# Gathering the rows of a mixture-of-experts stage by indirect DMA instead of by one-hot products

## The chip, the cores and the metric

The kernel runs as one program on one core of a Trainium2 chip. The metric is the device time of one execution in microseconds. Before the change three runs took 2869.97, 2870.82 and 2877.7 us, with a median of 2870.82 us.

## The reference, cut to what matters

The reference is two transformer-like blocks on 512 tokens of width 1024. The change touches only the last stage, the mixture of experts. Its routing picks two experts of 32 for each token, and only the chosen ones have a weight other than zero in `combine`:

```python
for e in range(N_EXPERTS):                       # 32 experts
    he = jax.nn.silu(t @ w_g[e]) * (t @ w_u[e])  # t: 512 x 1024, w_g and w_u: 1024 x 256
    out = out + combine[:, e:e + 1] * (he @ w_d[e])   # w_d: 256 x 1024
```

After it come the residual and a last normalisation. All inputs and outputs are float32. Each expert has 3 x 1024 x 256 weights, 3.15 MB, so the 32 experts have 100.7 MB that are read once.

## The kernel before, in words

The stage starts from two tiles that lie feature-major, `hT` (the residual) and `nT` (the normalised input of the experts), each 128 partitions by 8 blocks by 512 tokens. `tail2` (from L2257) computes the router's logits, and `choose` and `places` find for each token its two experts, their weights (`cmb`) and the token's place in each expert's list (`pos`, 0 to 63 for the 64 slots of an expert; an expert with more tokens is handled by `overflow`, under a condition that is read from the data). `token_major` transposes `nT` back to token-major on TensorE, and `split` (L2267 to L2270) turns each half of a block of 128 tokens into a high part `n2h` (ScalarE) and a remainder `n2l` (VectorE), both fp32r. `plain` does a plain copy of `hT` into `yac`, on which the experts' results are added.

`experts` (from L2073) runs over eight groups q of four experts. In each:

- Four VectorE comparisons make `oh`, a one-hot matrix of 512 tokens by 256 slots (L2081).
- The slots get their tokens' rows as a product: for each of eight feature blocks and four token blocks there is one matmul with `n2h` and one with `n2l` (L2093, L2094), 64 in all, with 256 columns each. `xg` receives the result from PSUM, two blocks at a time, half of the copies on ScalarE and half on VectorE (L2095). `xg` is double-buffered over q.
- Then two pairs of experts follow. In a pair the two experts stand beside each other in TensorE's columns (64 each). Four small matmuls with `chl` fetch the slots' weights (L2106), `w2` is made of them on VectorE, 16 fp32 matmuls that the trace shows as 32 instructions compute gate and up (L2118), then come Silu (L2122), four transposes of `oh` (L2125) and the copy `ohT`, the product with the weights `h` (L2128), two transposes of `h` (L2131) and the copy `hT` (L2133), and eight matmuls with the down weights (16 instructions, L2141). Their result is scaled and split into `yh` and `yl` (L2144 to L2146).
- At the end of the group, 32 matmuls with `ohT` (L2155, L2156) bring both pairs' results back to the tokens, and VectorE adds them to `yac` (L2157).

The weights come through `load` (L2053 on), in tiles of 1 MB, nine buffers (`EW`), and six tiles per pair: the first half of the rows of gate and up for each expert, the second half, and the down matrix. Tile j takes the buffer of tile j - 9: the first three tiles of a pair wait for the matmuls with down of the pair two before, the last three for the gate and up matmuls of the pair before. The DMAs are issued by SyncE, in program order, on one queue. In the gate and up loads partition p receives the rows k * 128 + p, so each run in memory is one row of 256 floats, 1 KB. A down row is 4 KB.

The order of instructions on each engine is chosen when the program is built, by a planner that goes by priorities (the order in the source) and by a timeline of its own. Every engine then executes its instructions in that order. PSUM has eight banks, here four of `pa`, three of `pb` and one of `pf`. TensorE instructions are called PE in the rows, VectorE DVE, ScalarE ACT, GpSimd POOL; SPq is SyncE's sequencer.

Of the kernel before, what the change touches and what calls it, by code (L numbers as in the profile page):

```python
# [20 lines left out]
D = 1024  # L21
# [9 lines left out]
L = 512  # L31
# [391 lines left out]
def constants():  # L423
    f = np.float32
    k = {"k_ident": np.eye(128, dtype=f)}
    s4 = np.zeros((128, 32), f)
    for j in range(4):
        s4[32 * j + np.arange(32), np.arange(32)] = 1
    k["k_sel4"] = s4
    t = np.arange(768)  # L430
    k["k_rst64"] = np.broadcast_to((t % 64 != 0).astype(f), (128, 768)).copy()
    dm = np.zeros((128, 2, 6, 32), f)
    s = np.arange(128)[:, None] % 32
    q = np.arange(32)[None, :]
# [35 lines left out]
    k["k_iota"] = np.broadcast_to(np.arange(64, dtype=f), (128, 64)).copy()  # L470
    inv = (10000.0 ** (-np.arange(0, 64, 2, dtype=np.float64) / 64)).astype(f)
    k["k_invf"] = np.tile(inv, 4)[:, None].copy()
    return k
# [1478 lines left out]
CAP = 64  # L1952
THR = CAP
EW = 9
GT = "pf"
G0 = "pa"


class Moe:
# [72 lines left out]
    def route(self, pool):  # L2032

        nc = self.nc
        t = lambda n, s: pool.tile([128, 4] + list(s), F32, name=n)
# [12 lines left out]
        self.chl = pool.tile([128, 4, 16, 2, 2], F32R, name="chl")  # L2048
# [4 lines left out]
    def load(self, i, ew, j):  # L2053


        nc = self.nc
        if j >= NE * 3 or j in self.ewt:
            return
        e, part = j // 6 * 2 + j % 2, j % 6 // 2
        t = ew.tile([128, 2048], F32, name="ew", bufs=EW).rearrange("p (k n) -> p k n", k=2 if part == 2 else 4)  # L2060
        rows = lambda w: i[w][0][e].rearrange("(k p) n -> p k n", p=128)
        if part < 2:
            for n, w in enumerate(("w_exp_gate_2", "w_exp_up_2")):
                nc.sync.dma_start(t[:, :, n * 256:n * 256 + 256], rows(w)[:, part * 4:part * 4 + 4])
        else:
            nc.sync.dma_start(t, rows("w_exp_down_2"))
# [6 lines left out]
    def experts(self, i, ew, n2h, n2l, yac, xg2, g2, yhl):  # L2073

        nc, tc = self.nc, self.tc
        with tc.tile_pool(name="eb", bufs=1, reuse_waits="tile") as eb:
            batch = []
            for q in range(8):
                oh = eb.tile([128, 4, 256], F32R, name="oh", bufs=2)
                for c in range(4):  # L2080
# [4 lines left out]
                xg = xg2[:, q % 2]  # L2085
                for k2 in range(4):
                    p = self.pt(GT if q else G0)
                    for kk in range(2):
                        k = k2 * 2 + kk
                        ks = slice(k * 128, (k + 1) * 128)  # L2090
                        o = p[:, kk * 256:kk * 256 + 256]
                        for c in range(4):
                            nc.tensor.matmul(o, n2h[:, c, ks], oh[:, c, :], start=(c == 0), stop=False)  # L2093
                            nc.tensor.matmul(o, n2l[:, c, ks], oh[:, c, :], start=False, stop=(c == 3))  # L2094
                    (nc.vector.tensor_copy if k2 % 2 else nc.scalar.copy)(  # L2095
                        xg[:, k2 * 2:k2 * 2 + 2, :], p.rearrange("p (a s) -> p a s", a=2))
                for pr in range(2):
                    e0 = q * 4 + pr * 2
                    for j in range(e0 * 3, e0 * 3 + 6):
                        self.load(i, ew, j)  # L2100
                    wts = [self.ewt.pop(j) for j in range(e0 * 3, e0 * 3 + 6)]
                    ss = slice(pr * 128, pr * 128 + 128)

                    pw = self.pt("pb")
                    for c in range(4):
                        nc.tensor.matmul(pw[:, :4], oh[:, c, ss], self.chl[:, c, e0 // 2].rearrange("p a b -> p (a b)"),  # L2106
                                         start=(c == 0), stop=(c == 3))
                    w2 = eb.tile([128, 1], F32, name="w2", bufs=2)
                    w4 = eb.tile([128, 4], F32, name="w4", bufs=2)
                    nc.vector.tensor_copy(w4, pw[:, :4])  # L2110
                    for x in range(2):
                        rs = slice(x * 64, x * 64 + 64)
                        nc.vector.tensor_add(w2[rs, :], w4[rs, x:x + 1], w4[rs, 2 + x:3 + x])

                    ph = self.pt("pa")
                    for k in range(8):
                        for x in range(2):
                            nc.tensor.matmul(ph[x * 64:x * 64 + 64, :], xg[:, k, pr * 128 + x * 64:pr * 128 + x * 64 + 64],  # L2118
                                             wts[k // 4 * 2 + x][:, k % 4, :], start=(k == 0), stop=(k == 7),
                                             tile_position=(0, x * 64))  # L2120
                    h = eb.tile([128, 256], F32, name="h", bufs=2)
                    nc.scalar.activation(h, ph[:, :256], AF.Silu)  # L2122
                    pt_ = self.pt("pb")
                    for c in range(4):
                        nc.tensor.transpose(pt_[:, c * 128:(c + 1) * 128], oh[:, c, ss].bitcast(F32), self.ident)  # L2125
# [109 lines left out]
class Tail:  # L2235
# [3 lines left out]
    def tail1(self, i, mo, mn, ys, x1d, g2d, ths):  # L2239
# [9 lines left out]
        for name, shape in (("tri8", [128, 64]), ("triu", [128, 128]), ("iota", [128, CAP_])):  # L2249
# [7 lines left out]
    def tail2(self, i, mo, out):  # L2257
        nc, tc = self.nc, self.tc
        rt = mo.tile([128, 4, 36], F32, name="rt")
        n2h, n2l = self.slot("n2h", "Q", True), self.slot("n2l", "A", True)  # L2260
        yac = self.slot("yac", "B", True, F32)
        self.ewt = {}
        with tc.tile_pool(name="ea", bufs=1, reuse_waits="tile") as ea:
# [1 line left out]
            logits = self.logits(i, mo, self.nT, rt)  # L2265

            def split(p, c, f):  # L2267
                fs = slice(f * 512, f * 512 + 512)
                nc.scalar.copy(n2h[:, c, fs], p)
                nc.vector.tensor_sub(n2l[:, c, fs], p, n2h[:, c, fs].bitcast(F32))  # L2270

            def plain(p, c, f):
                (nc.vector.tensor_copy if f else nc.scalar.copy)(yac[:, c, f * 512:f * 512 + 512], p)
# [16 lines left out]
            xg = self.mo.tile([128, 2, 8, 256], F32, name="xg", tag="P", bufs=1)  # L2290
            self.experts(i, ea, n2h, n2l, yac, xg, self.g2, yhl)
            self.finish(mo, yac, self.slot("yg", "Q", True, F32), self.fg, out)


# [256 lines left out]
```

## Time and profile before

| | |
|---|---|
| median of three runs | 2870.82 us |
| profiled execution, its own time | 2875.16 us |
| its span, first to last instruction | 2873.4 us |
| busy share of the span: PE, PEld, DVE, ACT, POOL | 95%, 73%, 54%, 35%, 9% |
| TensorE's mean granted clock | 0.98 |
| moved by DMA | 374.20 MB, mean 130 GB/s |
| loads of `ew` (gate, up: 64 DMAs of 512 KB each) | 9.9 and 8.8 us from issue to landing |
| loads of `ew` (down: 32 DMAs of 1024 KB) | 11.0 us from issue to landing |

PE is a matmul, PEld the load of its stationary operand, which overlaps with other matmuls. Matmuls overlap in the records, since they are pipelined: the distance between two starts, not the length of one, is what a matmul costs in a row of them. The expert stage is the last 350 us of the span; its PE is busy without a gap from 2525 to 2825 us.

### The profile page before, as it was taken

How to read it: one execution, taken by the hardware profiler on the slowest of the kernel's cores; microseconds unless marked ns; L12 is line 12 of the kernel's file. 1: busy time of each engine (PE TensorE's matmuls, PEld its weight loads, DVE VectorE, ACT ScalarE, POOL GpSimd, SP SyncE). 2: the span in 40 equal slices, each digit the busy share in tenths (PEclk: the TensorE clock that was granted, in tenths of full speed). 3: DMA queues.
4: the chain of work that ended last, by engine and by line, in shares of the span. 5: the costliest groups of instructions: out<-in, count | busy, mean ns of one | idle time of the engine just before them, and what ended most of it. 6: DMA issues, size and time to landing. Idle time of an engine off the chain costs nothing. (4 is left out here: it accounts for less than half of the span.)

```text
span 2873.4 us, 41502 instructions
## 1 busy us (share of the span) xinstructions
PE 2731.4 (95%) x16545; PEld 2099.0 (73%) x16546; DVE 1551.9 (54%) x3009; ACT 996.1 (35%) x1791; POOL 264.2 (9%) x303
## 2 busy tenths in 40 slices
PE   7999999999998878999999999999999999999997
PEld 5788888888787766688887778777667668854553
DVE  6333333348267995544345756676766654633334
ACT  5211111235235663322224424565444532311112
POOL 2000000002002220100000101121222220000000
PEclk9999999999999998999999999999999999999999
DMA  7422212224333237633324433202333475478885
GB/s 260 146 88 66 67 54 65 66 82 119 108 89 90 64 121 258 228 103 94 92 85 124 119 99 87 63 13 61 86 105 103 137 248 162 137 252 294 289 296 190
DMA packets 387125, 374.20 MB, mean 130 GB/s; under 512 B 20329, under 2 KB 316653, under 8 KB 386674
## 3 DMA queue, kind: packets, MB, share of 16 engines
q1 hardware_dynamic: 386930, 371.53, 41.2%
q8 instruction: 131, 2.15, 0.3%
q14 instruction: 64, 0.52, 0.1%
HBM read 343.94 MB, written 27.53 MB: 129 GB/s over the span
## 5 line engine op out<-in xcount | busy, mean ns | idle before, releaser
L191 ACT CAST whi<-wraw 128x1024 fp32r<-128x1024 f32 x277 | 285.9, 1042 | 748.2 <-PE pppa L211 333.5
L210 PE MATMUL pppa<-lath,whi 128*128 128x512 f32 (+4 forms) x1344 | 522.8, 390 | 19.2 <-ACT whi L191 5.7
L211 PE MATMUL pppa<-latl,whi 128*128 128x512 f32 (+3 forms) x1344 | 519.6, 387 | 5.7 <-DVE latl L358 3.6
L212 PE MATMUL pppa<-lath,wlo 128*128 128x512 f32 (+3 forms) x1344 | 513.6, 384 | 0.5 <-DVE wlo L192 0.4
L192 DVE TENSOR_TENSOR wlo<-wraw,whi 128x1024 fp32r<-128x1024 f32 (+1 forms) x273 | 332.7, 1225 | 253.8 <-ACT whi L191 249.2
L210 PEld LDWEIGHTS pppa<-lath,whi 128*128 128x128 f32 (+3 forms) x1344 | 253.0, 188 | 86.4 <-ACT whi L191 12.3
L211 PEld LDWEIGHTS pppa<-latl,whi 128*128 128x128 f32 (+2 forms) x1344 | 252.8, 188 | 65.9 <-DVE latl L358 6.0
L212 PEld LDWEIGHTS pppa<-lath,wlo 128*128 128x128 f32 (+2 forms) x1344 | 252.3, 188 | 56.5 <-issue 2.8
L211 PE MATMUL pppb<-hl,whi 128*128 128x512 f32 (+1 forms) x576 | 195.4, 341 | 0.0
L210 PE MATMUL pppb<-hh,whi 128*128 128x512 f32 (+1 forms) x576 | 193.4, 345 | 0.0
L212 PE MATMUL pppb<-hh,wlo 128*128 128x512 f32 (+1 forms) x576 | 191.6, 341 | 0.0
L416 DVE SCALAR_TENSOR_TENSOR xT<-pppb,sG,xT 128x512 f32<-128x512 f32 (+1 forms) x144 | 96.8, 690 | 138.2 <-PE pppb L212 138.1
L396 DVE TENSOR_TENSOR hf<-sg,pppa 128x256 f32<-128x256 f32 (+1 forms) x68 | 39.7, 584 | 234.7 <-PE pppa L212 233.4
L210 PE MATMUL pppf<-lath,whi 128*128 128x512 f32 x320 | 129.3, 404 | 5.0 <-ACT whi L191 1.7
L210 PE MATMUL pppa<-ctxh,whi 128*128 128x256 f32 (+1 forms) x440 | 124.8, 284 | 7.9 <-DVE W L918 7.9
L2118 PE MATMUL pppa<-ew,xg 128*64 128x512 f32 x512 | 131.2, 597 | 0.0
L210 PEld LDWEIGHTS pppb<-hh,whi 128*128 128x128 f32 x576 | 108.1, 189 | 28.0 <-issue 5.8
L212 PE MATMUL pppf<-lath,wlo 128*128 128x512 f32 x320 | 127.4, 398 | 0.6 <-DVE wlo L192 0.6
L211 PE MATMUL pppf<-latl,whi 128*128 128x512 f32 x320 | 127.7, 399 | 0.0
L211 PE MATMUL pppa<-ctxl,whi 128*128 128x256 f32 (+1 forms) x440 | 124.6, 283 | 0.2 <-POOL ctxl L356 0.2
L212 PE MATMUL pppa<-ctxh,wlo 128*128 128x256 f32 (+1 forms) x440 | 124.7, 283 | 0.0
L211 PEld LDWEIGHTS pppb<-hl,whi 128*128 128x128 f32 x576 | 108.5, 188 | 16.1 <-issue 3.4
(700 smaller groups left out, 5170.6 us busy)
## 6 DMA issues: line engine op xcount, KB each, us to landing
wraw<-in_ffn_w_dram SPq DMA_DIRECT2D x132, 512.0 KB, 4.1
wraw<-in_w_in_dram SPq DMA_DIRECT2D x102, 512.0 KB, 4.1
ew<-in_w_exp_gate_dram SPq DMA_DIRECT2D x64, 512.0 KB, 9.9
ew<-in_w_exp_up_dram SPq DMA_DIRECT2D x64, 512.0 KB, 8.8
ew<-in_w_exp_down_dram SPq DMA_DIRECT2D x32, 1024.0 KB, 11.0
mraw<-in_w_mod_dram SPq DMA_DIRECT2D x40, 512.0 KB, 6.6
wraw<-in_w_mod_dram SPq DMA_DIRECT2D x32, 512.0 KB, 4.4
mraw<-in_w_ada_dram SPq DMA_DIRECT2D x32, 512.0 KB, 6.7
```

The costliest lines, as they stand in the source:

```text
L191: nc.scalar.copy(hi[:, :n], raw[:, :n])
L192: (nc.gpsimd if pool else nc.vector).tensor_sub(lo[:, :n], raw[:, :n], hi[:, :n].bitcast(F32))
L210: nc.tensor.matmul(out, wh, xh, start=start, stop=False)
L211: nc.tensor.matmul(out, wh, xl, start=False, stop=False)
L212: nc.tensor.matmul(out, wl, xh, start=False, stop=stop)
L396: nc.vector.tensor_mul(h[:, :n], sg[:, :n], pp[1])
L416: nc.vector.scalar_tensor_tensor(x[:, o, :], p[:, :n], gate[:, o:o + 1], x[:, o, :], op0=OP.mult, op1=OP.add)
L2118: nc.tensor.matmul(ph[x * 64:x * 64 + 64, :], xg[:, k, pr * 128 + x * 64:pr * 128 + x * 64 + 64], wts[k // 4 * 2 + x][:, k % 4, :], start= ...
```

## The change

- `split` no longer makes a high part and a remainder. It copies each half block once (ScalarE for the first half, VectorE for the second) into one tile `n2`, with the features reordered on the way, so that feature p * 8 + k lies at k * 128 + p; the writes have a stride of 128 floats. After the second half SyncE stores the block's 128 rows in a DRAM tensor `n2d` (four stores of 512 KB).
- `chl` carries a third value per token besides the two parts of the weight: the token's number, from a new constant `tok`. The small matmuls with `oh` have six columns in place of four and so yield, for each of the 128 slots of a pair, the number of its token. VectorE turns it into an integer, `ix`, and GpSimd issues an indirect DMA which brings the 128 rows (4 KB each) from `n2d` into one of four slots of `xr`. This is `gather(q)`, for both pairs of a group; it is called one group ahead.
- `turn(n)` transposes the gathered rows of pair n in eight 128 by 128 pieces on TensorE into two PSUM banks (`pf` and `pb`), from where ScalarE and VectorE copy them to one of four slots of `xg4`. It stands in the source after the gate and up matmuls of the pair before.
- The 512 one-hot matmuls (L2093, L2094) and their copies are gone.
- In the gate and up loads partition p receives rows p * 8 to p * 8 + 7, four to a tile, so one run in memory is 4 KB. The down loads stay.

```diff
     def load(self, i, ew, j):
...
+            t = t.rearrange("p (n k m) -> p n k m", n=2, k=4)
             for n, w in enumerate(("w_exp_gate_2", "w_exp_up_2")):
-                nc.sync.dma_start(t[:, :, n * 256:n * 256 + 256], rows(w)[:, part * 4:part * 4 + 4])
+                nc.sync.dma_start(t[:, n], i[w][0][e].rearrange("(p k) n -> p k n", k=8)[:, part * 4:part * 4 + 4])
...
+            xr = self.slot("xr", "A", True, F32)
+            def gather(q):
+                oh = eb.tile([128, 4, 256], F32R, name="oh", bufs=2)
...
+                for pr in range(2):
+                    n = q * 2 + pr
+                    pw = self.pt("pb")
+                    for c in range(4):
+                        nc.tensor.matmul(pw[:, :6], oh[:, c, pr * 128:pr * 128 + 128],
+                                         self.chl[:, c, n].rearrange("p a b -> p (a b)"), start=(c == 0), stop=(c == 3))
+                    ix = eb.tile([128, 1], U32, name="ix", bufs=4)
+                    nc.vector.tensor_copy(ix, pw[:, 4:5])
+                    rows[n] = xr[:, n % 4, :]
+                    nc.gpsimd.indirect_dma_start(rows[n], None, n2d, bass.IndirectOffsetOnAxis(ap=ix, axis=0))
...
+            def turn(n):
+                r = rows.pop(n)
+                for f in range(2):
+                    p = self.pt(("pf", "pb")[f])
+                    for k in range(4):
+                        k4 = f * 4 + k
+                        nc.tensor.transpose(p[:, k * 128:(k + 1) * 128], r[:, k4 * 128:(k4 + 1) * 128], self.ident)
+                    (nc.vector.tensor_copy if f else nc.scalar.copy)(
+                        xg4[:, n % 4, f * 4:f * 4 + 4, :], p.rearrange("p (k s) -> p k s", k=4))
+            gather(0)
+            turn(0)
+            for q in range(8):
+                if q < 7:
+                    gather(q + 1)
...
-                for k2 in range(4):
-                    p = self.pt(GT if q else G0)
-                    for kk in range(2):
...
-                            nc.tensor.matmul(o, n2h[:, c, ks], oh[:, c, :], start=(c == 0), stop=False)
-                            nc.tensor.matmul(o, n2l[:, c, ks], oh[:, c, :], start=False, stop=(c == 3))
-                    (nc.vector.tensor_copy if k2 % 2 else nc.scalar.copy)(
-                        xg[:, k2 * 2:k2 * 2 + 2, :], p.rearrange("p (a s) -> p a s", a=2))
...
                     nc.scalar.activation(h, ph[:, :256], AF.Silu)
+                    if e0 < 30:
+                        turn(e0 // 2 + 1)
...
             def split(p, c, f):
-                fs = slice(f * 512, f * 512 + 512)
-                nc.scalar.copy(n2h[:, c, fs], p)
-                nc.vector.tensor_sub(n2l[:, c, fs], p, n2h[:, c, fs].bitcast(F32))
+                (nc.vector.tensor_copy if f else nc.scalar.copy)(
+                    n2[:, c, :].rearrange("p (k q) -> p q k", k=8)[:, f * 64:f * 64 + 64, :],
+                    p.rearrange("p (q k) -> p q k", k=8))
+                if f:
+                    nc.sync.dma_start(n2d[c * 128:(c + 1) * 128, :], n2[:, c, :])
```

## Rows read from the trace of the kernel before

**Rows 1.** The page: busy us (share of the span) and instructions of each engine.
```profile
PE 2731.4 (95%) x16545; PEld 2099.0 (73%) x16546; DVE 1551.9 (54%) x3009; ACT 996.1 (35%) x1791; POOL 264.2 (9%) x303
```
**Rows 2.** Chain that ended last, in the stage: start us, us, what, count.
```profile
2540.65 0.52 PE pppb L2125 x4
...
2590.61 6.87 PE pppa L2118 x32
...
2632.69 6.87 PE pppa L2118 x32
...
2838.43 6.89 PE pppa L2118 x32
```
**Rows 3.** SyncE's waits in the stage: waited for: us in total, times, longest.
```profile
SPq L2064 <- PE pppa L2141: 124.9, 14, 15.2
```
**Rows 4.** Windows: from:to, length, busy us of engines, PEclk, DMA share, GB/s.
```profile
2565.00:2573.00 8.00, 8.00 (x28) 2.38 (x25) 1.72 (x3) 0.00 (x0) 0.00 (x0) 1.00 1.09 349
2575.00:2580.00 5.00, 5.00 (x29) 4.31 (x28) 2.07 (x3) 0.59 (x1) 0.00 (x0) 1.00 1.02 398
2583.00:2591.00 8.00, 8.00 (x55) 5.21 (x55) 4.15 (x12) 2.38 (x4) 0.00 (x0) 1.00 0.02 8
```
**Rows 5.** Timeline of SyncE's issues: start us, us, engine, line, operation, count.
```profile
2571.06 2.88 SPq L2066 DMA_DIRECT2D ew<-in_w_exp_down_dram  x2
...
2574.84 0.51 SPq L2064 DMA_DIRECT2D ew<-in_w_exp_up_dram  x1
2590.63 0.37 SPq L2064 DMA_DIRECT2D ew<-in_w_exp_gate_dram  x1
```
**Rows 6.** Timeline of PE, one-hot products: the first and the fourteenth of a row.
```profile
2585.21 0.28 PE L2093 MATMUL pppf<-oh,n2h 128*128 128x256 f32 x1
...
2586.75 0.28 PE L2094 MATMUL pppf<-oh,n2l 128*128 128x256 f32 x1
```
**Rows 7.** Groups by line: engine, operation, shapes, count, busy us, mean ns, idle before.
```profile
L2093 PE MATMUL pppf<-oh,n2h 128*128 128x256 f32 x224 | 56.6, 290 | 0.0
L2094 PE MATMUL pppf<-oh,n2l 128*128 128x256 f32 x224 | 55.1, 283 | 0.0
...
L2270 DVE TENSOR_TENSOR n2l<-pppa,n2h 128x512 fp32r<-128x512 f32 x8 | 5.4, 686 | 0.0
```
**Rows 8.** Timeline of PE: a pair's gate and up, and its down.
```profile
2546.47 7.04 PE L2118 MATMUL pppa<-ew,xg 128*64 128x512 f32 x32
...
2558.57 3.65 PE L2141 MATMUL pppa<-ew,hT 128*64 128x512 f32 x16
```
**Rows 9.** Timeline of DVE: the first comparisons; `hT` of the same pair.
```profile
2519.10 2.77 DVE L2081 TENSOR_TENSOR oh<-pos,iota 128x256 fp32r<-128x256 f32 x8 [1.75 <-DVEq L2166]
...
2555.84 0.42 DVE L2133 COPY hT<-pppb 128x256 f32<-128x256 f32 x1 [1.37 <-PE pppb L2131]
```
**Rows 10.** Timeline of PE at the stage's start.
```profile
2519.68 0.55 PE L2093 MATMUL pppa<-oh,n2h 128*128 128x256 f32 x1 [3.44 <-DVE oh L2081]
...
2521.52 0.21 PE L2106 MATMUL pppb<-chl,oh 128*128 128x4 f32 x1
...
2530.39 5.37 PE L2118 MATMUL pppa<-ew,xg 128*64 128x512 f32 x24
```
**Rows 11.** Timeline of ACT at the start.
```profile
2526.17 1.28 ACT L2095 ACT_TABLE_LOAD   x1 [14.21 <-PE pppa L2094]
2527.47 0.59 ACT L2095 COPY xg<-pppa 128x512 f32<-128x512 f32 x1
```
**Rows 12.** Windows of 5 us at the start.
```profile
2520.00:2525.00 5.00, 5.00 (x26) 5.00 (x26) 1.88 (x6) 0.00 (x0) 0.00 (x0) 0.50 0.00 0
2525.00:2530.00 5.00, 5.00 (x43) 5.00 (x43) 0.69 (x1) 2.46 (x3) 0.00 (x0) 0.98 0.02 3
```
**Rows 13.** Landings: the result's stores; of L2064, the loads of gate and up.
```profile
out_dram<-yg SPq DMA_DIRECT2D x4, 512.0 KB, 3.5
...
DMA to landing us min/median/max: 5.7/8.8/12.9
```

More of the change, by code (lines that the diff above doesn't have):

```diff
@@ L470, in constants @@
     k["k_iota"] = np.broadcast_to(np.arange(64, dtype=f), (128, 64)).copy()
+    k["k_tok"] = (np.arange(4)[None, :] * 128 + np.arange(128)[:, None]).astype(f)
     inv = (10000.0 ** (-np.arange(0, 64, 2, dtype=np.float64) / 64)).astype(f)
@@ L1954 @@
 EW = 9
-GT = "pf"
-G0 = "pa"
 class Moe:
@@ L2046, in route @@
         nc.vector.tensor_tensor(self.cov, self.cov, self.cmb, op=OP.mult)
-        self.chl = pool.tile([128, 4, 16, 2, 2], F32R, name="chl")
+        self.chl = pool.tile([128, 4, 16, 3, 2], F32R, name="chl")
+        nc.vector.tensor_copy(self.chl[:, :, :, 2, :], self.tok[:, :, None, None].to_broadcast([128, 4, 16, 2]))
         cv = self.cmb.rearrange("p c (a b) -> p c a b", b=2)
@@ L2059, in load @@
         e, part = j // 6 * 2 + j % 2, j % 6 // 2
-        t = ew.tile([128, 2048], F32, name="ew", bufs=EW).rearrange("p (k n) -> p k n", k=2 if part == 2 else 4)
-        rows = lambda w: i[w][0][e].rearrange("(k p) n -> p k n", p=128)
+        t = ew.tile([128, 2048], F32, name="ew", bufs=EW)
         if part < 2:
+            t = t.rearrange("p (n k m) -> p n k m", n=2, k=4)
             for n, w in enumerate(("w_exp_gate_2", "w_exp_up_2")):
-                nc.sync.dma_start(t[:, :, n * 256:n * 256 + 256], rows(w)[:, part * 4:part * 4 + 4])
+                nc.sync.dma_start(t[:, n], i[w][0][e].rearrange("(p k) n -> p k n", k=8)[:, part * 4:part * 4 + 4])
         else:
-            nc.sync.dma_start(t, rows("w_exp_down_2"))
+            t = t.rearrange("p (k n) -> p k n", k=2)
+            nc.sync.dma_start(t, i["w_exp_down_2"][0][e].rearrange("(k p) n -> p k n", p=128))
         self.ewt[j] = t
@@ L2071, in prefetch, with experts @@
             self.load(i, ew, j)
-    def experts(self, i, ew, n2h, n2l, yac, xg2, g2, yhl):
+    def experts(self, i, ew, n2d, yac, xg4, g2, yhl):
         nc, tc = self.nc, self.tc
@@ L2077, in experts @@
             batch = []
-            for q in range(8):
+            ohs, w2s, rows = {}, {}, {}
+            xr = self.slot("xr", "A", True, F32)
+            def gather(q):
                 oh = eb.tile([128, 4, 256], F32R, name="oh", bufs=2)
+                ohs[q] = oh
                 for c in range(4):
@@ L2084, in experts @@
                         self.iota[:, None, :].to_broadcast([128, 4, CAP]), op=OP.is_equal)
-                xg = xg2[:, q % 2]
-                for k2 in range(4):
-                    p = self.pt(GT if q else G0)
-                    for kk in range(2):
[L2089 to L2092, printed above, removed]
-                            nc.tensor.matmul(o, n2h[:, c, ks], oh[:, c, :], start=(c == 0), stop=False)
-                            nc.tensor.matmul(o, n2l[:, c, ks], oh[:, c, :], start=False, stop=(c == 3))
-                    (nc.vector.tensor_copy if k2 % 2 else nc.scalar.copy)(
-                        xg[:, k2 * 2:k2 * 2 + 2, :], p.rearrange("p (a s) -> p a s", a=2))
+                for pr in range(2):
[8 more added lines that the diff above has]
+                    nc.gpsimd.indirect_dma_start(rows[n], None, n2d, bass.IndirectOffsetOnAxis(ap=ix, axis=0))
+                    w2 = w2s[n] = eb.tile([128, 1], F32, name="w2", bufs=4)
+                    w4 = eb.tile([128, 4], F32, name="w4", bufs=2)
+                    nc.vector.tensor_copy(w4, pw[:, :4])
+                    for x in range(2):
+                        rs = slice(x * 64, x * 64 + 64)
+                        nc.vector.tensor_add(w2[rs, :], w4[rs, x:x + 1], w4[rs, 2 + x:3 + x])
@@ L2097, in experts @@
+            gather(0)
[3 more added lines that the diff above has]
+                    gather(q + 1)
+                oh = ohs.pop(q)
                 for pr in range(2):
@@ L2102, in experts @@
                     ss = slice(pr * 128, pr * 128 + 128)
[L2104 to L2113, printed above, removed]
+                    xg, w2 = xg4[:, (q * 2 + pr) % 4], w2s.pop(q * 2 + pr)
                     ph = self.pt("pa")
@@ L2117, in experts @@
                         for x in range(2):
-                            nc.tensor.matmul(ph[x * 64:x * 64 + 64, :], xg[:, k, pr * 128 + x * 64:pr * 128 + x * 64 + 64],
-                                             wts[k // 4 * 2 + x][:, k % 4, :], start=(k == 0), stop=(k == 7),
+                            nc.tensor.matmul(ph[x * 64:x * 64 + 64, :], xg[:, k, x * 64:x * 64 + 64],
+                                             wts[k // 4 * 2 + x][:, :, k % 4, :], start=(k == 0), stop=(k == 7),
                                              tile_position=(0, x * 64))
@@ L2248, in tail1 @@
         self.residual(i, mo, mh, ml, x1d, self.hT, self.nT)
-        for name, shape in (("tri8", [128, 64]), ("triu", [128, 128]), ("iota", [128, CAP_])):
+        for name, shape in (("tri8", [128, 64]), ("triu", [128, 128]), ("iota", [128, CAP_]), ("tok", [128, 4])):
             t = mo.tile(shape, F32, name=name)
@@ L2259, in tail2 @@
         rt = mo.tile([128, 4, 36], F32, name="rt")
-        n2h, n2l = self.slot("n2h", "Q", True), self.slot("n2l", "A", True)
+        n2 = self.slot("n2", "Q", True, F32)
+        n2d = self.dr.tile([L, D], F32, name="n2d")
         yac = self.slot("yac", "B", True, F32)
@@ L2289, in tail2 @@
             yhl = self.mo.tile([128, 2, 2, D], F32R, name="yhl", tag="H", bufs=1)
-            xg = self.mo.tile([128, 2, 8, 256], F32, name="xg", tag="P", bufs=1)
-            self.experts(i, ea, n2h, n2l, yac, xg, self.g2, yhl)
+            xg = self.mo.tile([128, 4, 8, 128], F32, name="xg", tag="P", bufs=1)
+            self.experts(i, ea, n2d, yac, xg, self.g2, yhl)
             self.finish(mo, yac, self.slot("yg", "Q", True, F32), self.fg, out)
```

## The prediction, made before the change was run

> **What bounds the kernel now.** The page comes first: PE is busy for 95% of the span, POOL for 9% [rows 1]. An average says nothing of one stage, so I go to the chain that ended last, in the expert stage. From one group's second gate-and-up block (2590.61) to the next's (2632.69) it takes 42.08 us, and the chain lies on PE throughout [rows 2]. The windows ask whether DMA could be behind it: for 8 of those 42 us DMA moves 8 GB/s while PE works all 8 [rows 4]. SyncE's timeline shows why: after 2574.84 no load of gate or up goes out before 2590.63 [rows 5], and the waits name what holds them, the down matmuls that free the buffers, 124.9 us in 14 waits [rows 3]. So PE sets the pace and DMA follows it, but not from far: a group's 12.58 MB of weights (four experts: 16 loads of 512 KB for gate and up, 8.39 MB, and four of 1024 KB for down, 4.19) take 24.0 us at the 349 GB/s of the 1 KB runs and 10.5 us at the 398 of the 4 KB runs [rows 4], 34.6 in 42.1. A saving on PE of more than 7.5 us per group would meet the old stream.
>
> **One-hot products out.** Fourteen of them start 2585.21 to 2586.75, 13 steps, so one costs 0.118 us in a row; the listed mean of 283 to 290 ns is the pipelined length [rows 6, 7]. A group has 64: 7.6 us. Seven groups (224 of each kind [rows 7]) lie on the path behind the first gate-and-up block: 448 x 0.118 = 52.9 us off. The first group's 64 belong to the start, below.
>
> **Transposes in.** Eight per pair; four transposes of the same size took 0.52 us on the chain [rows 2], so 1.04 us per pair. Fifteen pairs (the first belongs to the start): 15.6 us on. The small matmuls number the same, with six columns for four: nothing. The copies out of PSUM are four per group as before, and run beside PE.
>
> **The gap that the one-hot products filled.** Gate and up of a pair end at 2553.5, `hT` is ready at 2555.84 + 0.42 = 2556.26, and down starts at 2558.57 [rows 8, 9]. Silu, product, transposes and copy thus need about 2.8 us in which PE must have other work, and one-hot products stood there for the most part. After the change the transposes of the next pair (1.0 us), those of `oh` (0.5) and the products back to the tokens are left to fill it. Bounds: everything covered, 0; only 1.5 of 2.8 us covered in each of 15 pairs, 1.3 x 15 = 19.5. The products back to the tokens are there in most groups, so I take 0.5 us each, nearer the low end: 7.5 us on.
>
> **The start.** Before, the first comparison is at 2519.10 and gate and up start at 2530.39, 11.3 us later [rows 9, 10]. In their place come: four of the eight comparisons (half of 2.77 us), 1.4; four small matmuls at 0.21 each at the half clock, 0.8; the integer copy, 0.2; GpSimd's issue and the gather's landing; four transposes at about 0.2, 0.8; the table load and the copy on ScalarE, 1.28 + 0.59 [rows 10, 11]. That is 5.1 us without the gather. The trace has no indirect DMA. The nearest rows: a 512 KB store on an idle queue, 3.5 us; the slowest 512 KB load of gate or up under full traffic, 12.9 [rows 13]. DMA is idle there (0 GB/s from 2520 [rows 12]), so I take a value near the low end, 6 with GpSimd's part: 11.1 us, as before. Two things come on top. PE warms up later: it was granted 0.50, the 1.2 GHz level, from 2520 to 2525, after it had stood nearly idle, and 0.98 in the next 5 us [rows 12]; that slow stretch fell on one-hot products and now falls on gate and up, some 4 us at half speed, +2. And the four stores to `n2d`, 2.1 MB, share the queue with the first nine weight tiles: 5.3 us at 398 GB/s, mostly in front of the route's end, +1. On the other side `split` loses four VectorE instructions of 0.69 us [rows 7], if a strided write costs what a plain one does: 0 to -2.8. I take +3, bounds -3 to +13 (the gather at 12.9 instead of 6, and the stores not covered at all).
> *The Trainium skill's GPSIMD Engine Reference, section "2.1 Instruction dispatch", has a rule against this change: the first call of freshly loaded code on GpSimd pays some 6 us for loading it. No row here shows one (POOL's other work is ordinary). By it the start would be +9, inside those bounds, and the time 6 us above the sum.*
>
> **The stream.** The gathers add 16 x 0.52 MB, so a group moves 13.63 MB. If all 4 KB runs go at 398 GB/s, this takes 34.2 us [rows 4]. PE's new period is 42.1 - 7.6 + 2.1 + 1.0 = 37.6 us: PE still bounds, with 3.4 us to spare. The run length thus gives nothing by itself; it keeps DMA from taking over, since with 1 KB runs (24.0 + 5.24 MB / 398 = 13.2) the stream would need 37.2. The gathers are issued one group ahead, with at least some 20 us for their landing of 12.9 at worst [rows 13]; on SyncE only the four stores are new, before the loop, and behind a store that waits for its copy stand weight loads that are first needed 20 us later.
>
> **The sum.** -52.9 + 15.6 + 7.5 + 3 = -26.8 us. The profiled execution took 2875.2 us, 4.3 above the median of the runs; against its own time the sum gives 2848.4, against the median 2870.8 - 26.8 = 2844. This I forecast. Its own bounds: -52.9 + 15.6 + 0 - 3 = -40.3, so 2830; -52.9 + 15.6 + 19.5 + 13 = -4.8, so 2866.
>
> **Rivals.** *DMA takes over.* The 4 KB windows may be fast only because they are short, or the gathered rows disturb the stream. At the 349 GB/s of the longer window 13.63 MB take 39.1 us per group: seven periods save 7 x 3.0 = 21 and the start gives 3 back, 2853. For it: the DMA share above 1 in both windows; against it: the down rows, which the change copies in form, already flow at 398 between slower ones [rows 4].
> *The Trainium skill, DMA: Bandwidth & Descriptors, section "Where 436 GB/s comes from", says that reads from HBM are bound at about 358 GB/s per core. By that, 38.1 us per group would be the floor, and 7 x 4.0 - 3 = 25 us the saving, 2846; the measured 398 does not agree with the rule, and I go by the measurement; its chance is part of this rival's.*
>
> *GpSimd becomes the bound, and the kernel slower.* An indirect DMA of 128 rows needs an address for each row, and nothing in the trace prices that. Two gathers per group go through one queue, and each transpose in PE's fixed order stands ahead of the transposes of `oh`, of down, and of all behind. Up to 18.8 us per gather it stays hidden behind 37.6 us; the group is slower than before from 21 us on, 0.16 us per row. At 24 us: 7 x (48 - 42.1) + 18 more at the start = 59 on, 2930. Against it: a store of 512 KB, its 128 rows and all, lands in 3.5 us [rows 13], and POOL is idle in 91% of the span [rows 1]. The same end is reached if the planner sets the small matmuls of `gather` late, so that PE waits 8 us for each group's first gather: 45.6 per group, 2870.8 + 25 + 3 = 2899.
>
> *The change does not shorten the stage*, because DMA was the bound all along: 2871 to 2874. The idle 8 us with PE full speak against it [rows 4].
>
> *More than forecast.* The chain has costs where PE changes between 64-column and 128-column work. If fewer one-hot pieces also mean fewer changes, 2 us more per group go: 2830 or a little below.
>
> **How the numbers follow.** Forecast 0.66, DMA takes over 0.15, more than forecast 0.09, a late or slow gather 0.06, no shortening 0.04. The range must leave out no more than 2 in 10; from 2826 to 2864 it holds the forecast but for the worst sum of all bounds, the DMA case, and most of the case of more. About 0.3%, 8.6 us, is what a measurement of this kernel can tell from no change. Faster by more than that: nearly all of the first three cases, 0.89. Within: the end of the gap and start bounds with the last case, 0.05. Slower: 0.06.
>
> **What would show it.** Right: no one-hot products on the chain, gate-and-up to gate-and-up of the next group at 36 to 39 us; PE full in the stage's windows, with DMA at or over 360 GB/s on the mean; first gate and up at 2530 to 2537; POOL a few us per gather; waits of PE for `xr` near nothing. Wrong: PE waiting for `ew` in every group (the stream bounds), for `xr` (the gather bounds), windows in which the 4 KB runs stay under 360 GB/s, or a first gate-and-up block later than 2545.

## The result, and the profile after

| | before | after |
|---|---|---|
| median, same chip | 2874.26 us (4 runs) | 2847.56 us (4 runs) |
| ratio, 95% interval | | 0.9892 [0.9875, 0.9908] |
| median, timed a second time | 2875.33 us (9 runs) | 2842.43 us (4 runs) |
| ratio, 95% interval | | 0.9885 [0.9870, 0.9900] |
| profiled execution: own time, span | 2875.16, 2873.4 us | 2847.28, 2845.5 us |

The change is faster by 1.1%. The forecast was 2844 us by the median and 2848.4 by the profiled execution, from a sum of -26.8 us; the profiled pair differs by -27.9.

The page of the kernel after, its busy engines and GpSimd's queue, against [rows 1]:

```profile
PE 2684.1 (94%) x16161; PEld 2052.9 (72%) x16162; DVE 1553.9 (55%) x3022; ACT 995.2 (35%) x1787; POOL 280.4 (10%) x319
...
q0 software_dynamic: 2304, 8.39, 0.8%
```

PE has 47 us less work, and the queue of the gathers (packets, MB, share) appears. The chain of waits after, in the loop, against [rows 2] (start us, us, what):

```profile
2557.46 6.92 PE pppa L2137 x32
2593.70 6.87 PE pppa L2137 x32
2630.75 6.87 PE pppa L2137 x32
...
2810.30 6.89 PE pppa L2137 x32
```

These are the second gate-and-up blocks of the groups, the same place as L2118 before. A group takes 36.2, 37.1 and so on, on the mean of seven (2557.46 to 2810.30) 36.1 us; before it was 41.7 (2546.63 to 2838.43). The windows over exactly these seven periods, first of the kernel before, then of the one after (from:to, length, busy us of PE, PEld, DVE, ACT, POOL, PEclk, DMA share, GB/s):

```profile
2546.63:2838.43 291.80, 290.86 (x1455) 153.30 (x1452) 108.37 (x216) 38.00 (x69) 0.00 (x0) 1.00 0.88 300
```
```profile
2557.46:2810.30 252.84, 245.72 (x1131) 112.75 (x1128) 107.26 (x222) 37.92 (x68) 11.23 (x12) 1.00 0.97 373
```

Length minus the first busy time is PE's idle time: 0.94 us before, 7.1 after. So the loop is 39.0 us shorter, 45.1 by less work on PE and 6.2 the other way by PE standing still. What PE stands still for, and what SyncE waits for ([rows 3] before), in the same stretch (waited for: us, times, longest):

```profile
PE pppa L2162 <- DVE hT L2154: 5.9, 11, 0.6
PE pppb L2152 <- DVE h L2149: 1.0, 1, 1.0
```
```profile
SPq L2065 <- PE pppa L2162: 103.4, 14, 10.4
```

PE waits for `hT`, never for `ew` or `xr`; SyncE still waits for PE. The stream runs behind PE, at up to 424 GB/s (windows of 2 us, after):

```profile
2574.00:2576.00 2.00, 2.00 (x10) 0.55 (x6) 0.00 (x0) 0.00 (x0) 0.00 (x0) 1.00 1.02 418
...
2580.00:2582.00 2.00, 2.00 (x8) 0.66 (x7) 0.69 (x1) 0.00 (x0) 0.00 (x0) 1.00 1.04 424
```

The start went the other way. Three timelines after, with what ended an idle time in brackets: the last stores of the rows on SyncE, the first comparisons on VectorE, gathers on GpSimd; and the chain from there:

```profile
2517.34 1.58 SPq L2295 DMA_DIRECT2D n2d<-n  x2
```
```profile
2521.89 0.13 DVE L2041 CAST cnti<-mx 1x1 int32<-1x1 f32 x1
...
2528.86 2.77 DVE L2088 TENSOR_TENSOR oh<-pos,iota 128x256 fp32r<-128x256 f32 x8 [6.84 <-SPq L2187]
```
```profile
2532.57 1.17 POOL L2102 DMA_INDIRECT xr<-n2d,ix  x1 [202.27 <-DVE w L2108]
...
2588.39 0.94 POOL L2102 DMA_INDIRECT xr<-n2d,ix  x1 [45.97 <-DVE w L2105]
```
```profile
2528.86 2.77 DVE oh L2088 x8
...
2532.57 4.55 DMA xr<-n2d,ix
...
2537.16 1.11 PE pppf L2117 x4
2538.28 0.85 PE pppb L2117 x4
2539.13 1.50 PE pppb L2096 x8
2540.63 6.02 PE pppa L2137 x16
...
2547.12 3.58 PE pppa L2137 x16
```

The last stores go out at 2517.34, the counts from which the branch is decided (`cnti`) are ready at 2522.0, and yet the first comparison starts only at 2528.86: VectorE waits 6.84 us for SyncE's sequencer at the branch (L2187), where it waited 1.75 before [rows 9]. Meanwhile the transfers that stand on the queue run on at 422 GB/s and come to their end just ahead of the comparison (windows of 2 us, after):

```profile
2522.00:2524.00 2.00, 0.00 (x0) 0.00 (x0) 0.02 (x1) 0.00 (x0) 0.00 (x0) 0.50 1.03 422
2524.00:2526.00 2.00, 0.00 (x0) 0.00 (x0) 0.00 (x0) 0.00 (x0) 0.00 (x0) 0.50 0.79 320
2526.00:2528.00 2.00, 0.00 (x0) 0.00 (x0) 0.00 (x0) 0.00 (x0) 0.00 (x0) 0.50 0.12 49
```

The rest of the program repeats less well than the stage: in the profiled run after, the stage's first weight load goes out 4.3 us later (2462.77 for 2458.43), with a granted clock of 0.91 in four stretches of 20 us ahead of it where before had 0.97 to 1.00; in the second profile of this same kernel it goes out at 2455.0, and in the other runs it stands anywhere up to 2469.6. So I set every profile's times against its own first weight load of the stage:

| us after the first weight load | first comparison | first gate and up | second block | loop of 7 groups | end of span |
|---|---|---|---|---|---|
| before | 60.7 | 72.0 | 88.2 | 291.8 | 415.0 |
| after | 66.1 | 77.8 | 94.7 | 252.8 | 382.7 |
| after, second time | 65.1 | 76.6 | 93.2 | 252.8 | 381.3 |
| e1, runs only | 63.5 | 74.4 | 90.7 | 291.8 | 417.5 |
| e2, gathers only | 65.1 | 76.7 | 94.1 | 252.8 | 382.2 |
| e3, half of down | 66.7 | 78.4 | 95.5 | 259.3 | 390.0 |
| e4, six tiles | 65.7 | 77.4 | 94.5 | 252.8 | 382.6 |
| e5, three tiles held | 61.0 | 76.9 | 93.2 | 254.0 | 382.5 |
| e6, copies on ScalarE | 65.8 | 77.5 | 94.1 | 249.9 | 379.3 |
| e7, products back later | 65.3 | 76.9 | 93.3 | 249.4 | 378.0 |
| e8, late gather | 65.2 | 77.3 | 91.6 | 328.9 | 455.7 |
| e10, held for the turn | 61.0 | 72.7 | 90.6 | 252.1 | 378.0 |
| e11, e6 and e7 | 65.1 | 76.8 | 92.1 | 247.7 | 375.1 |
| e12, all three | 61.1 | 72.7 | 88.5 | 246.8 | 370.5 |

In the profiled pair the stage lost 6.5 us up to the second block, won 39.0 in the loop and is 32.2 shorter; the 4.3 ahead of it, which are not the change's, leave the 27.9. The second block is no clean cut between the two kernels: after, two and a half of the fifteen turns stand ahead of it, and before, 32 of the 448 one-hot products. From the first gate-and-up block to the last, which has them all, it is 308.0 us before (88.2 - 72.0 + 291.8) and 269.7 after, 38.3 less.

### The profile page after: what moved, and what is told of

Its sections match the earlier page's. It is cut to its first block, busy times and chain, and to the rows that moved or that the text cites. A ratio compares the mean times of both kernels' runs of the same rounds, so it can differ in the third digit from the quotient of the medians.

```text
span 2845.5 us, 40809 instructions
## 1 busy us (share of the span) xinstructions
PE 2684.1 (94%) x16161; PEld 2052.9 (72%) x16162; DVE 1553.9 (55%) x3022; ACT 995.2 (35%) x1787; POOL 280.4 (10%) x319
## 3 DMA queue, kind: packets, MB, share of 16 engines
q1 hardware_dynamic: 338498, 373.62, 40.7%
## 5 line engine op out<-in xcount | busy, mean ns | idle before, releaser
L212 PEld LDWEIGHTS pppa<-lath,wlo 128*128 128x128 f32 (+2 forms) x1344 | 252.1, 188 | 55.5 <-issue 2.5
```

The costliest lines, as they stand in the source:

```text
L212: nc.tensor.matmul(out, wl, xh, start=False, stop=stop)
```

## The experiments

**Runs of four rows alone (e1).** The one-hot products of before, with the new loads; the features are put in the new order by `split`.

```diff
-                nc.sync.dma_start(t[:, :, n * 256:n * 256 + 256], rows(w)[:, part * 4:part * 4 + 4])
+                nc.sync.dma_start(t[:, n], i[w][0][e].rearrange("(p k) n -> p k n", k=8)[:, part * 4:part * 4 + 4])
```

> The old one-hot products and high and low parts stay (with the features reordered in the split), only the weights come in 4 KB runs. Theory (PE set the pace before, the stream only followed): the time from one group's second gate-and-up block to the next stays at 41 to 42 us, DMA only stands idle longer (from 8 to about 12 us per group), total within 4 us of the kernel before; the strided writes of the split may cost up to 5 us once. Rival (the stream was a good part of the bound): 41 to 42 falls by 1.5 us or more per group, the total by over 10 us.

2883.3 us, ratio 1.0009 [0.9993, 1.0024]. The loop has the same 291.8 us to the hundredth, and SyncE waits longer for PE (136.5 us in 14 waits in place of 124.9). PE was the bound, and the new loads give nothing by themselves. The median is 4.8 us above that of the kernel before on the same chip (2878.51), where I had allowed 4; the first comparison comes 2.8 us later, and here sixteen copies of `split` write with a stride.

**Gathers alone (e2).** The changed kernel with the loads and the copies of `split` as before.

```diff
-                    n2[:, c, :].rearrange("p (k q) -> p q k", k=8)[:, f * 64:f * 64 + 64, :],
-                    p.rearrange("p (q k) -> p q k", k=8))
+                    n2[:, c, f * 512:f * 512 + 512], p)
```

> The gathers and transposes stay, the weights come in 1 KB runs again and the features lie in their old order. Theory (at 349 GB/s for 8.39 MB and 420 for 5.24 MB the stream needs 24.0 + 12.5 = 36.5 us per group and PE 36.1, so the two together no longer fit): 37.5 to 39.5 us per group, PE waiting for ew, 8 to 22 us slower than the changed kernel, still 5 to 20 faster than before. Rival (the run length has no part in it): 36.1 us per group and the time of the changed kernel.

2845.65 us, ratio 0.9897 [0.9876, 0.9917]: the whole gain, with the old runs. The windows of e2 show why the stream doesn't take over: the seven periods, 8 us of 1 KB runs, and 2 us with down rows among them.

```profile
2549.71:2802.51 252.80, 245.70 (x1130) 112.76 (x1128) 107.20 (x222) 37.93 (x68) 11.23 (x12) 1.00 1.01 373
2565.00:2573.00 8.00, 8.00 (x28) 2.38 (x26) 1.40 (x3) 0.00 (x0) 0.00 (x0) 1.00 1.08 382
...
2576.00:2578.00 2.00, 2.00 (x10) 1.60 (x9) 1.51 (x3) 0.00 (x0) 0.00 (x0) 1.00 1.05 423
```

The same runs that moved at 349 GB/s before [rows 4] move here at 382, and the mean is the 373 of the kernel after. DMA's share is 1.01, so it is full, but it is not late: SyncE waits 100.9 us for PE. Why the old kernel's window stood at 349 is open.

**Half of the down weights (e3).** The second expert of a pair uses the first one's down weights, so 2.1 of 13.6 MB per group are not loaded.

```diff
+        if part == 2 and j % 2:
+            self.ewt[j] = self.ewt[j - 1]
+            return
```

> As the changed kernel, but the second expert of each pair uses the first one's down tile and its own is not loaded: 2.1 MB of 13.63 less per group. Theory (PE still sets the pace, with a DMA share of 0.97 that is only full because buffers come free at that pace): 35.5 to 36.1 us per group, the total not more than 5 us faster. Rival (the stream is already the bound): 4 to 5 us less per group, 25 to 35 us faster.

2854.72 us, ratio 0.9921 [0.9900, 0.9942]. Over its seven periods, with 299 GB/s in place of 373, nothing is won:

```profile
2556.44:2815.69 259.25, 252.14 (x1131) 113.02 (x1128) 107.48 (x222) 37.92 (x68) 11.24 (x12) 1.00 0.83 299
```

PE stands still for the same 7.1 us as after, and never for `ew`, so the stream is no bound. The loop is 6.4 us longer (five of its periods have 37.4 us), all of it in PE's work, though the work is that of the kernel after: with other loads the planner set it in another order. In that order every second gate-and-up block is cut into the same five pieces as in the kernel before (under e7). Counting each PE instruction from its start to the start of the next, gate and up take 4.7 us more than after, the products back to the tokens 1.7 more, and every other kind of work is the same to 0.1 us.

**Six tiles ahead of the branch (e4).** In the source the prefetch ends after six tiles.

```diff
-        for j in range(EW):
+        for j in range(6):
```

> As the changed kernel, but six of the nine weight tiles are asked for before the condition of the overflow branch, the other three with the second pair. Theory (the branch is left only when SyncE's outstanding transfers have landed, and the stores of the rows stand behind 9.4 MB of weights): the wait in front of the first comparison falls from 6.8 to 1.5 to 3 us, first gate and up 4 to 6 us earlier, total 3 to 6 us faster than the changed kernel. Rival (the wait is the branch's own, or the gather's data has to wait for the same traffic anyway): no change within 2 us.

2847.86 us, ratio 0.9901 [0.9879, 0.9923]. The planner issued the same nine tiles ahead of the branch all the same, so this says nothing on the start.

**Three tiles held back (e5, e10).** A small copy into the tile, from a value that exists only after the branch, makes tiles 6 to 8 wait: in e5 for the first gather's weights, in e10 for the copy of the first turn. The diff is that of e10; in e5 the copy covers the gate half alone, so that an up load of the held tiles still goes early.

```diff
+        if after is not None:
+            nc.vector.tensor_copy(t.rearrange("p (n m) -> p n m", n=2)[:, :, 0], after.to_broadcast([128, 2]))
...
             turn(0)
+            for j in range(6, EW):
+                self.load(i, ew, j, xg4[:, 0, 0, 0:1])
```

> Three of the nine weight tiles are issued only after the first gather's weights are there, so 6 tiles and the four stores of the rows (8.4 MB in place of 11.5) are on the queue ahead of the branch; all else is the changed kernel. Theory: the 5 us by which the first comparison of the stage came later (66.1 us after the first weight load in the changed kernel, 60.7 before) are a wait at the branch for transfers under way, at 404 to 424 GB/s, so 3.1 MB less end it 7 us sooner: the first comparison stands at 60.5 to 62 us after the first weight load, the run takes 4 to 5 us less than the changed kernel, 2842 to 2844. Rival: the branch waits for the route (the counts), not for transfers: the first comparison stays at 65 to 66 and the time at 2847. Third: what is gained there is lost when the three late tiles are needed by the second pair: PE waits for ew, time 2847 or above.

> As in the run that holds three weight tiles back, but until the first turn's copy is there, so that they are on the queue neither ahead of the branch nor beside the first gather. Theory: the wait at the branch is for transfers under way (gone with 3.1 MB less, first comparison at 61.0 us after the first weight load), and what took it back was the gather's landing, 8.76 us beside the late tiles in place of 4.55: here both are short, the first gate and up starts 72 to 74 us after the first weight load in place of 77.8, and the run takes 4 to 5 us less than the changed kernel on the same chip. Rival: the gather takes 8 us or more for another cause (its first use, the stores still under way), and the first gate and up stays at 76 to 78: no gain. Third: the tiles come too late for the second pair, 3.1 MB or 7.5 us at 415 GB/s from 2540 on, and PE waits for ew there.

e5: 2846.02 us, ratio 0.9889 [0.9871, 0.9907]; e10: 2842.85, 0.9892 [0.9873, 0.9910], where the changed kernel has 2842.43 on the chip of e10. In both the wait at the branch is gone, and the first comparison stands at 61.0, as in the kernel before. VectorE's timeline in e10:

```profile
2518.78 2.77 DVE L2090 TENSOR_TENSOR oh<-pos,iota 128x256 fp32r<-128x256 f32 x8 [1.80 <-SPq L2191]
```

In e5 the gain is lost at once, at the first gather (chain of e5):

```profile
2534.31 8.76 DMA xr<-n2d,ix
```

In e10 the first gather is short again and the first gate and up comes 3.9 us earlier, as expected; but then the next gather needed stands behind the held tiles (chain of e10):

```profile
2522.48 4.53 DMA xr<-n2d,ix
...
2532.65 11.39 DMA xr<-n2d,ix
...
2544.18 0.63 PE pppf L2119 x4
```

1.4 us are lost there. By the table 3.3 remain at the end of the span, against the kernel's second profile. The medians do not show it: the runs of e10 lie between 2838.75 and 2853.18.

**Both copies of a turn on ScalarE (e6).**

```diff
-                    (nc.vector.tensor_copy if f else nc.scalar.copy)(
+                    nc.scalar.copy(
```

> Both copies of a turn run on ScalarE; all else is the changed kernel. Theory: PE's 7 us of idle time in the loop are its wait for hT, and hT is late because its copy stands on VectorE behind a copy of a turn (0.69 us) and the comparisons of the next group: with the copy gone the waits for hT fall from 5.9 us in all to 3 or less, time 2 to 4 us under the changed kernel. Rival: hT is late by its own chain (Silu, product, transposes), which ScalarE's second copy lengthens: the waits stay at 6 or more, time 2847 to 2851.

2839.39 us, ratio 0.9867 [0.9849, 0.9885]. Waits in the loop:

```profile
PE pppa L2162 <- DVE hT L2154: 3.4, 9, 0.5
PE pppa L2162 <- issue: 1.0, 2, 0.5
PE pppb L2152 <- DVE h L2149: 0.4, 1, 0.4
```

The wait for `hT` falls from 5.9 to 3.4 us, not quite to 3, and the loop is 2.9 us shorter: 2.2 less standing still, 0.7 less work. So `hT` was late in part because its copy stood on VectorE behind the turn's. The chain of after shows what else stands there, the turn's copy, the comparisons and then `hT`:

```profile
2601.63 0.69 DVE xg L2118
2602.32 1.34 DVE oh L2088 x4
2603.66 0.34 DVE hT L2154
```

In the chain of e6 the comparisons stand straight ahead of `hT` once in five of the seven groups, so a part of the rest is theirs; how much, no run isolates.

**Products back to the tokens later (e7).**

```diff
-                for c in range(4):
+                with self.later(100 if q < 7 else 0):
+                  for c in range(4):
```

> The products back to the tokens get a later priority, so that by the order on TensorE the stage has 66 changes between 64- and 128-column matmuls in place of 88; the work is the same. Theory: a change costs some 0.4 to 0.5 us (four interruptions of a gate and up block make 9.30 us of 6.92), and of the gain of the change 7 us come from 18 changes that went with the one-hot products: 22 fewer here give 8 to 11 us, the run takes 2837 to 2840. Rival: the pieces are slow for another cause (they wait for something that the profile does not show, the weights' transfer or PSUM), and it moves along with them: 2845 to 2849. Third: the products back to the tokens are missed where they covered the wait for hT: PE idles 0.5 us or more per pair, and the gain is 0 to 4.

2838.39 us, ratio 0.9874 [0.9854, 0.9893]. The loop is 3.4 us shorter (PE's busy time 242.2 for 245.7), where 22 changes fewer should have given 8 to 11. So the price is not one per change. What a change costs is seen in the chain of before at an interrupted block, and in the chain of after at another:

```profile
2606.86 4.44 PE pppa L2118 x20
2611.30 0.67 PE pppb L2155 x2
2611.96 1.00 PE pppa L2118 x2
...
2616.50 1.86 PE pppa L2118 x6
```
```profile
2681.26 4.43 PE pppa L2137 x18
...
2686.36 1.01 PE pppa L2137 x4
```

In an undisturbed block one instruction costs 6.87 / 32 = 0.215 us. Two should cost 0.43 and cost 1.00, six 1.29 and cost 1.86: 0.57 too much. Twenty should cost 4.30 and cost 4.44, only 0.14 too much. Where in the block the piece stands does not decide this: eighteen at the head of a block cost as much as twenty, and two in the midst as much as four. What decides is the number. A matmul is two instructions here, and the matmuls of the pair's two experts, which stand beside each other in TensorE's columns, follow each other in turn. A piece of 4, 8, 16 or 20 instructions has both experts' matmuls in equal number, and in none of the fourteen traces does it cost more than 0.15 too much, by PE's starts. A piece of 2, 6, 14 or 18 has one matmul without its neighbour, and each such piece costs 0.52 to 0.57 too much: its single matmul takes as long as two neighbours together, 0.43 more than its share, and the rest is near the 0.14 of the others. So an interruption between two neighbours is the dear one, since it leaves an odd piece on either side. That the two run at the same time is my reading of these times; no run moves these interruptions alone. I count 28 such odd pieces in the loop before (four in each of seven groups), 20 after, 20 in e7, and 28 in e3, whose gate and up take 4.7 us more than after. So e7 left the number of the dear ones as it was and took away cheap ones.

**No lead for the gather (e8).** One buffer for the one-hot matrix, the next group's gathers only in the second pair, its first turn right behind.

```diff
-                oh = eb.tile([128, 4, 256], F32R, name="oh", bufs=2)
+                oh = eb.tile([128, 4, 256], F32R, name="oh", bufs=1)
...
-                if q < 7:
-                    gather(q + 1)
...
                     nc.scalar.copy(ohT, pt_)
+                    if pr == 1 and q < 7:
+                        gather(q + 1)
+                        turn(e0 // 2 + 1)
```

> The comparisons and gathers of the next group are issued only in the second pair of a group, after the last use of the one-hot matrix, and its first turn comes straight after; the work is the same. Theory: a gather is 0.94 us on GpSimd and 4.4 to 6.8 to land, behind the integer copy; one turn per group is now waited for, some 7 to 8 us in which PE has only 2.8 us of other work, and there are 18 more changes between 64 and 128 columns: 4 to 5 us plus 1 us per group, period 41 to 42, time 2880 to 2890, about as slow as the kernel before. Rival: the planner and the pair's other work cover most of it: under 2 us per group, time under 2862.

2921.94 us, ratio 1.0160 [1.0140, 1.0181]: slower than the kernel before, and by far more than I had expected. PE's wait in six groups of e8, then windows of one of them, and of all seven periods:

```profile
PE pppf L2117 <- DMA xr<-n2d,ix: 48.5, 6, 8.6
```
```profile
2555.00:2565.00 10.00, 2.43 (x16) 1.74 (x13) 1.37 (x9) 0.38 (x1) 1.88 (x2) 0.76 1.03 420
2565.00:2575.00 10.00, 10.00 (x46) 4.87 (x46) 3.70 (x6) 2.41 (x4) 0.00 (x0) 0.89 0.67 255
```
```profile
2548.80:2877.73 328.93, 271.51 (x1151) 126.78 (x1148) 110.72 (x235) 39.14 (x70) 13.15 (x14) 0.90 0.79 291
```

8.1 us per group are waited, with DMA full at 420 GB/s beside it, and PE's granted clock, 1.00 in the loop after, is 0.76 of full speed in that stretch and 0.89 in the next. A group takes 47.0 us on the mean of seven, 10.9 more than after: 7.2 more of standing still, and 3.7 more for PE's work (271.5 us for 245.7 in the loop), in part by the clock, in part because the order has the 28 odd pieces of the kernel before.

**The two gains together (e11), and all three (e12).**

> The changed kernel as it is, timed once more beside the three other runs, so that differences of a few us are taken on one chip. Both theories: 2845 to 2849, the first gate and up 77 to 78 us after the first weight load of the stage, a mean loop period of 36.1 us.

> Both copies of a turn on ScalarE, and the products back to the tokens at a later priority. Alone, the first took 2.9 us of the seven loop periods and the second 3.4. Theory: they are separate terms (PE's wait for hT, and changes between 64- and 128-column work), so together 5 to 7 us less in the loop than the changed kernel, 2840 to 2843 by the time. Rival: they share the same gap (with the products later, hT is covered by them), and both together give no more than 3.5.

> All three edits: copies on ScalarE, products back later, three tiles held until the first turn. Theory: the sum, 9 to 12 us below the changed kernel on the same chip, 2835 to 2839, ratio to the kernel before 0.986 to 0.988 or lower. Rival: the planner's order with the held tiles brings back the interruptions of gate and up, 5 us below at most.

On one chip: the changed kernel (e9) 2842.43 us, ratio 0.9885 [0.9870, 0.9900], below the 2845 to 2849 that I had expected, with the same loop of 252.8 us; e11 2834.60, 0.9866 [0.9847, 0.9885]; e12 2833.48, 0.9855 [0.9839, 0.9870]. The loop of e11 is 5.1 us shorter than after, of 2.9 + 3.4 = 6.3: mostly separate terms. e12 is the best of these versions; by its profile its stage ends 10.8 to 12.2 us before that of the changed kernel, 9.0 by the medians, and its interval only just touches that of e9.

## Why the prediction was right, and where by luck

- **PE was the bound, DMA followed.** Right: e1 leaves the loop unchanged, e2 gives the whole gain with the old loads, in e3 less is moved and PE stands still as long, and SyncE waits for PE after as before.
- **One-hot products out, transposes in.** From the first gate-and-up block to the last the terms are -52.9 + 15.6 + 7.5 = -29.8 us. Measured are -38.3, with 2.4 in them for the half clock in the first block, which I had put to the start; without it -40.7, 10.9 better than the terms. By PE's starts, each instruction counted to the next one's, the 448 one-hot products cost 56.2 us (0.126 each for 0.118), the fifteen turns 13.6 (0.91 each for 1.04), gate and up 4.6 less than before, and the gap below 1.3 less than I took; the small rest takes 0.3 back. The products back to the tokens cost the same as before (59.6 for 60.1). The 4.6 are the rival "more than forecast", at a third of its size (0.7 us per group, not 2): eight odd pieces fewer at 0.57. That the order does this e3 shows: the order of before in those blocks, with the work of after, takes the 4.7 back.
- **The gap.** 0.5 us per pair, 7.5 us, against 6.2 measured. The mechanism was incomplete: I priced PE's missing cover alone, but `hT` is also later on VectorE, behind a turn's copy and the comparisons, and e6 gave back 2.5 of the wait.
- **The stream.** I held the 1 KB runs for a limit that the new loads had to lift, 37.2 us per group, above the 36.1 that came out. e2 refutes this step: run length plays no part. And 398 GB/s was too low for the new runs, which reach 424.
*The Trainium skill, DMA: Bandwidth & Descriptors, section "Where 436 GB/s comes from", puts the HBM side at about 358 GB/s per core and says that it binds; the loop's mean of 373 and its windows at 418 to 424 do not agree with that. The same section puts a measured 425 GB/s near the fabric's rate, and with this the windows agree.*
- **The gather.** 0.94 us on GpSimd, and 4.4 to 6.8 us from its start to the landing (16 of them), against 6 taken for both; hidden, since it is issued about 12 us ahead (2588.39, for the turn at 2600.49), not the 20 that I had read. e8 shows that this lead decides: the rival "late gather" was priced at 45.6 us per group and 2899 us, and measured 47.0 and 2922. Its wait of 8 us was right; I had left out that PE's own work takes longer beside it (the clock of 0.90 over the loop, and the order).
*The rule in the GPSIMD Engine Reference of the Trainium skill, section "2.1 Instruction dispatch", a first call of freshly loaded code that costs some 6 us, is not seen: the first gather takes 1.17 us on GpSimd, later ones 0.94, and it lands 4.55 us after its start. Whether its code was freshly loaded the trace does not tell.*
- **The start.** +3 forecast, +8.2 measured: the first gate-and-up block starts 5.8 us later (77.8 for 72.0; on the span at 2540.6, past the 2530 to 2537 that I had named, 4.3 of it ahead of the stage), and its half clock costs 2.4 (6.02 us for sixteen instructions that later take 3.58). Right: comparison to first gate and up, 11.7 us for the 11.1 worked out, and the half clock, for which I took 2. Wrong is the step that put the four stores at +1, "mostly in front of the route's end": their 2.1 MB make 11.5 MB with the nine tiles, the queue is not empty at the branch, and the branch waits for it, 5.1 us more (4.1 in the second profile, by a wait of 5.81). e5 and e10 show this: with the three tiles held back the wait is gone. Whether the branch waits for all of the queue or for the stores alone, which stand last on it, these runs do not tell apart. `split` saved nothing that is seen: the counts are ready 59.2 us after the first weight load, before 58.9.

So the sum of -26.8 met the -27.9 of the profile by luck, because errors cancel: from the first gate-and-up block to the last, the half clock aside, 10.9 us better than the terms, the start 5.2 worse, 4.3 ahead of the stage and 0.3 behind the last block. Without the 4.3 the change is worth 32 to 34 us, which is also what the second timing gives (32.9).

## What to carry to other kernels

Work that PE does only to move rows can go to an indirect DMA where it can be issued far enough ahead: here 12 us of lead made a 1.1% gain, and none made a 1.6% loss. When work leaves an engine whose order is planned, count what it did besides: the cover that it gave to a chain on other engines, and the interruptions that it caused, above all those that part two matmuls which stand beside each other. And look at what stands on the queue where a program branches: here the branch was left only when the transfers under way had ended.

## What the hardware showed that I had not expected

- A copy from PSUM whose writes have a stride of 128 floats costs 1.06 us on ScalarE and 1.02 on VectorE; the same copies with plain writes in e2 cost 0.57 and 0.68. I had taken the same price. Groups by line, after and then e2:

```profile
L2291 ACT COPY n<-pppa 128x512 f32<-128x512 f32 x4 | 4.0, 1060 | 0.1
...
L2291 DVE COPY n<-pppa 128x512 f32<-128x512 f32 x4 | 4.0, 1022 | 0.0
```
```profile
L2289 DVE COPY n<-pppa 128x512 f32<-128x512 f32 x4 | 2.7, 683 | 0.0
...
L2289 ACT COPY n<-pppa 128x512 f32<-128x512 f32 x4 | 2.3, 574 | 0.6 <-PE pppa L1948 0.6
```

- A gather's landing follows the queue that it meets: from GpSimd's start it took 4.5 us alone, 8.76 and 11.39 beside the held weight tiles (e5, e10), and for the ones that PE waited for 7.5 to 8.5 in e8's full stream.
- Where two matmuls of 64 columns stand beside each other, a piece that has one of them without the other costs some 0.57 us too much in these kernels, a piece of whole pairs at most 0.15: two instructions of such a block take 1.00 us, as four do, and eighteen 4.43, as twenty do.
